# Layer 1's modulation rows issued in every third turn of layer 0's feed-forward network

## The chip, the cores and the metric

The kernel runs on one core of a Trainium2 chip. The metric is device time in microseconds (us) of one execution; the time quoted for the kernel before is the median of three runs.

PE is the matrix engine, PEld its weight loads, DVE the vector engine, ACT the scalar engine, POOL the general engine, and SP the engine whose queue issues the transfers between device memory and on-chip memory. Each engine works through its own list of instructions in order and waits for the others by semaphores. A "granted clock" of 1.00 is PE's full speed.

## The reference

Two transformer layers work on 512 latent tokens and 256 context tokens of width 1024, in float32. Each layer first makes six modulation vectors (shift, scale and gate, for the attention and for the feed-forward network), then runs attention and a feed-forward network with squared ReLU:

```python
for i in range(DEPTH):                                  # DEPTH = 2
    mod_x = jax.nn.silu(c) @ w_ada[i] + b_ada[i]        # c: 1024, w_ada[i]: 1024 x 6144
    mod_c = jax.nn.silu(c_ctx) @ w_ada[i] + b_ada[i]
    sh1, sc1, g1, sh2, sc2, g2 = jnp.split(mod_x[:, None, :], N_MOD, axis=-1)
    ...
    hx = x * (1.0 + sc1) + sh1
    hc = ctx * (1.0 + csc1) + csh1
    ax, ac = ...                                        # windowed attention, differential attention
    x = layer_norm(alpha * x + g1 * ax, ln1_g[i], ln1_b[i])
    fx = sqrelu_mlp(x * (1.0 + sc2) + sh2, mlp_w1[i], mlp_w2[i])
    x = layer_norm(alpha * x + g2 * fx, ln2_g[i], ln2_b[i])
    if need_ctx: ...                                    # the same for the context, layer 0 only
return x
```

The modulation vectors of layer 1 depend on nothing but `c`, `c_ctx`, `w_ada` and `b_ada`, so they can be made at any time before layer 1 wants them.

## The kernel before, in words

**Matrix products.** Every float32 product is made of three products of rounded operands: a weight tile `w` is split by ACT into a high part (`w_h`, a rounding copy, L264) and by DVE into a low part (`w_l = w - w_h`, L314), and `mm3` (L325 to L327) multiplies high by high, low by high and high by low. So each weight tile passes through four engines: SP loads it into a `w_raw` tile, ACT casts it, DVE subtracts, PE uses it. There are three `w_raw` tiles in the ring `rraw` (`NRAW = 3`) for layer 0.

**Layer 0's feed-forward network** (`mlp_pipe`) treats 768 tokens in six blocks of 128. The first product goes in sixteen "pairs" q of 256 hidden columns; from q = 3 on each pair takes seven half-size products of twelve matmuls (384 columns wide, tile `h_ps`; their weights are called `w_half`). Between these products stands the second product in small pieces: a "group" (tile `y_ps`) is one chunk c of hidden columns, one half of the output columns and one token block, and it is done in two half groups of six matmuls (512 columns wide). `steps(n)` lets n half groups run. Before q = 3 there are twelve, in each pair q = 3 to 13 twelve (4, 4, 4, 0), and in q = 14 and 15 six each.

**The filler.** `steps` calls `R.extra()` once after each half group, and `ahead()` calls it once in each pair. Those calls are named turns below: 12 + 11 x 12 + 2 x 6 = 156 from the half groups and 13 from the pairs, 169 in all. In layer 0 a turn takes the next step of the generator `filler`, which is `ada_rows`: it makes modulation vectors without PE. A step loads two rows of 128 x 512 of the transposed `w_ada` into a `w_raw` tile (tensor `in_w_adaT`, one 512 KB transfer), and DVE multiplies each with a broadcast copy of silu(c) (tile `cB`) and sums along the row (`tensor_tensor_reduce`, in the trace CUSTOM_DVE_ANT_0 with a DVE_READ_ACCUMULATOR2_ANT behind it). The last gate of layer 0 and the two vectors that layer 1's attention wants first are made for both latent and context tokens: such a piece has four of these DVE instructions ("double piece" below), the other vectors' pieces have two ("single piece"). The width is done in two halves; each half has one step that loads `cB`, then 12 double pieces, then 16 single pieces: 2 x (1 + 12 + 16) = 58 steps, with 160 DVE instructions.

When a gate vector is complete (m = 2 or 5), `ada_gate` turns it into rows: PE transposes it (`gate_t`, L456), ACT copies it (`gate_s`), SP stores it (`gate_d`). What the turns have not done is done where it is wanted: `need(...)` runs the generator on, in `g2` for layer 0's last gate, in `done2` for the first two vectors of layer 1, and after the whole feed-forward network for the rest of layer 1.

**What sets the order.** PE's order is written by a planner in the kernel (`Flow`): it keeps model times for the other engines and takes the job whose inputs are ready by that model. The other engines' orders, SP's too, come from the scheduler of the framework, which goes by program order and the tiles that are free. In the hardware each of these lists is worked off strictly in order, so a transfer that waits for a `w_raw` tile holds up all transfers behind it on SP, and a DVE instruction that waits for its transfer holds up all behind it on DVE.

Of the kernel before, what the change touches and what calls it, by code (L numbers as in the profile page):

```python
# [234 lines left out]
def hybrid_block(ctx: ExitStack, tc: tile.TileContext, t: dict, out: bass.AP):  # L235
# [373 lines left out]
    def tok_product(pool, src, W, seq, acc, gates, done=None, st=None, scale=1.0, extra=None, pre={}, sink=None,  # L609
# [5 lines left out]
        for i, (half, tb) in enumerate(seq):  # L615
# [41 lines left out]
            if extra is not None and tb < 4:  # L657
                next(extra, None)
# [802 lines left out]
    with tc.tile_pool(name="mlp0", bufs=1, reuse_waits="tile") as pool:  # L1461
# [26 lines left out]
        class R0:  # L1488
            rhalf = Ring(fl, 3)
            mixes = ((2, 2, 2, 0), (4, 4, 4, 0))  # L1490
            p3_first, gate_at, res = True, 16, None
            ahead, done = 1, 0

            def pair_raws(self):
                return [(x, None, None) for x in self.raws]
# [29 lines left out]
                    dma(D, [], out=acc[tb], in_=m_spill[tb])  # L1525

            def extra(self):
                next(filler, None)

        def main0():  # L1530
            yield from tok_product(pool, oT, {1: st1["W"]}, [(1, tb) for tb in range(NTB)], acc, (gx, gc), done1, st1,
# [42 lines left out]
        filler = ada_rows(pool, c_rows.rearrange("s k p -> s (k p)"))  # L1574
# [359 lines left out]
    with tc.tile_pool(name="mlp1", bufs=1, reuse_waits="tile") as pool:  # L1934
# [37 lines left out]
        class R1:  # L1972
            rhalf = Ring(fl, 4)
            mixes = ((1, 1, 1, 1), (2, 2, 2, 2))
            p3_first, gate_at, ahead = True, 10, 2
# [110 lines left out]
```

## Time and profile before

| | us |
|---|---|
| median of three runs (1687.13 to 1692.9) | 1690.02 |
| the profiled execution | 1690.94 |
| its span, first to last instruction | 1689.1 |
| PE busy | 1578.0 (93% of the span) |
| DVE busy | 1131.7 (67%) |
| ACT busy | 792.2 (47%) |
| POOL busy | 445.6 (26%) |
| mean granted PE clock | 0.975 |

The profile comes from one execution. Its page gives the busy time of each engine, the span in 40 slices of 42 us (each digit a busy share in tenths, with the granted PE clock and the share of the DMA engines below), and the chain of waits. Other views group the waits, list instructions in order of time, or give the busy times of chosen stretches; a row "(x158)" in such a stretch counts instructions. Matmuls overlap in the records, so PE can be shown busy throughout and yet do fewer of them: their count in a stretch says more than the busy time. Some matmul records can be missing (a few per cent).

### The profile page before, as it was taken

What the parts mean: (1) busy time and instruction counts of PE and PEld (TensorE: products, weight loads), DVE (VectorE), ACT (ScalarE), POOL (GpSimd) and SP (SyncE); (2) the same over time, 40 slices, a digit from 0 to 9 for tenths busy, and PEclk for the clock granted to TensorE, in tenths of its full rate; (3) what the DMA queues carried; (4) which work ended last, traced back from release to release, by engine and by line L of the source; (5) the groups of instructions that cost most, each with busy time, mean ns of one, the idle gap of its engine ahead of it and who ended that gap; (6) DMA issues with size and microseconds to landing.
All of it is one profiled execution on the core that took longest, in us unless ns stands there. A gap on an engine that the chain in (4) does not pass through costs nothing. (4 is left out here: it accounts for less than half of the span.)

```text
span 1689.1 us, 25129 instructions
## 1 busy us (share of the span) xinstructions
PE 1578.0 (93%) x9465; PEld 1388.1 (82%) x9465; DVE 1131.7 (67%) x2204; ACT 792.2 (47%) x1683; POOL 445.6 (26%) x364
## 2 busy tenths in 40 slices
PE   7899999999687899999999899999989899999997
PEld 5787777789576799899888899899877788999986
DVE  4655677698889864453567677777664975566687
ACT  3465675364222243342425555555552645555550
POOL 1333454114111112111281122220100023333463
PEclk9999999999798899999999999999999899999998
DMA  9111541543765722121143222211114233332331
GB/s 367 40 51 32 190 161 39 193 147 103 235 213 167 232 89 75 50 95 55 50 146 116 60 69 69 66 51 38 48 50 150 63 125 100 100 100 100 100 101 50
DMA packets 66433, 181.16 MB, mean 107 GB/s; under 512 B 7368, under 2 KB 13320, under 8 KB 66312
## 3 DMA queue, kind: packets, MB, share of 16 engines
q1 hardware_dynamic: 66312, 179.56, 31.6%
q8 instruction: 74, 1.21, 0.3%
q14 instruction: 47, 0.39, 0.1%
HBM read 168.49 MB, written 11.04 MB: 106 GB/s over the span
## 5 line engine op out<-in xcount | busy, mean ns | idle before, releaser
L325 PE MATMUL y_ps<-w_h,hid 128*128 128x512 f32 (+1 forms) x648 | 256.7, 396 | 27.3 <-ACT w_h L264 26.3
L326 PE MATMUL y_ps<-w_l,hid 128*128 128x512 f32 (+1 forms) x648 | 257.0, 397 | 10.1 <-DVE w_l L314 10.1
L327 PE MATMUL y_ps<-w_h,hid 128*128 128x512 f32 (+1 forms) x648 | 255.0, 394 | 0.0
L268 POOL TENSOR_TENSOR w_sum<-w_raw 128x512 f32<-128x512 f32 x52 | 94.8, 1822 | 501.5 <-DMA w_raw<-in_w 435.5
L314 DVE TENSOR_TENSOR w_l<-w_raw,w_h 128x1024 fp32r<-128x1024 f32 (+1 forms) x133 | 163.3, 1237 | 73.3 <-ACT w_h L264 72.7
L264 ACT CAST w_h<-w_raw 128x1024 fp32r<-128x1024 f32 (+1 forms) x133 | 131.7, 1001 | 146.7 <-PE y_ps L327 68.4
L325 PEld LDWEIGHTS y_ps<-w_h,hid 128*128 128x128 f32 x648 | 124.6, 192 | 52.4 <-ACT w_h L264 28.2
L260 DVE TENSOR_TENSOR w_half<-w_raw,w_half 128x512 fp32r<-128x512 f32 x130 | 103.9, 803 | 86.3 <-ACT w_half L264 86.0
L326 PEld LDWEIGHTS y_ps<-w_l,hid 128*128 128x128 f32 x648 | 124.5, 192 | 34.7 <-DVE w_l L314 12.7
L327 PEld LDWEIGHTS y_ps<-w_h,hid 128*128 128x128 f32 x648 | 124.5, 192 | 26.2 <-DVE hid L260 0.3
L264 ACT CAST w_half<-w_raw 128x512 fp32r<-128x512 f32 x130 | 79.8, 619 | 125.9 <-PE h_ps L327 75.4
L325 PE MATMUL qkv_ps<-w_h,hx 128*128 128x384 f32 (+1 forms) x384 | 128.9, 336 | 0.6 <-ACT qT L264 0.5
L326 PE MATMUL qkv_ps<-w_l,hx 128*128 128x384 f32 (+1 forms) x384 | 123.6, 322 | 0.0
L327 PE MATMUL qkv_ps<-w_h,hx 128*128 128x384 f32 (+1 forms) x384 | 123.5, 322 | 0.0
L260 DVE TENSOR_TENSOR fx<-y_ps,fx 128x512 f32<-128x512 f32 x110 | 75.6, 687 | 68.9 <-PE y_ps L327 68.5
L268 POOL TENSOR_TENSOR e<-e,sm 128x512 f32<-128x512 f32 (+2 forms) x96 | 92.6, 977 | 108.6 <-DVE sm L260 90.0
L264 ACT ACTIVATE relu<-relu 128x384 f32<-128x384 f32 (+3 forms) x104 | 69.5, 671 | 50.9 <-DVE relu L260 49.5
L268 POOL TENSOR_TENSOR rope<-rope,rope 128x256 f32<-128x256 f32 (+1 forms) x40 | 34.5, 862 | 213.5 <-DVE rope L260 170.0
L260 DVE CUSTOM_DVE_ANT_0 w_raw<-w_raw,cB 128x512 f32<-128x512 f32 x112 | 77.0, 725 | 12.5 <-DMA w_raw<-in_w_adaT 12.4
L264 ACT ACTIVATE e<-e,nm 128x513 f32<-128x513 f32 (+2 forms) x96 | 65.9, 687 | 32.8 <-DVE nm L260 26.0
L264 ACT COPY relu<-h_ps 128x384 f32<-128x384 f32 (+1 forms) x78 | 32.8, 421 | 92.9 <-PE h_ps L327 92.3
L325 PE MATMUL h_ps<-hx1m,w_half 128*128 128x256 f32 x260 | 73.0, 281 | 3.0 <-ACT relu L264 2.8
(266 smaller groups left out, 4280.4 us busy)
## 6 DMA issues: line engine op xcount, KB each, us to landing
w_raw<-in_w SPq DMA_DIRECT2D x128, 512.0 KB, 3.6
w_raw<-in_w_adaT SPq DMA_DIRECT2D x56, 512.0 KB, 4.5
w_raw<-in_w_ada SPq DMA_DIRECT2D x24, 512.0 KB, 4.3
w_raw<-in_b_w SPq DMA_DIRECT2D x32, 384.0 KB, 3.5
raw<-in_w_ada SPq DMA_DIRECT2D x16, 512.0 KB, 9.6
w_raw<-in_a_wq SPq DMA_DIRECT2D x8, 512.0 KB, 4.8
w_raw<-in_a_wo SPq DMA_DIRECT2D x8, 512.0 KB, 4.3
w_raw<-in_b_wo SPq DMA_DIRECT2D x8, 512.0 KB, 4.5
```

Source lines behind the costliest of these rows:

```text
L260: fn(**kw)
L264: fn(**kw)
L268: fn(**kw)
L314: last["split"] = nc.vector.tensor_tensor(**kw)
L325: nc.tensor.matmul(out=o, lhsT=lh, rhs=rh, start=start, stop=False, **kw)
L326: nc.tensor.matmul(out=o, lhsT=lh, rhs=rl, start=False, stop=False, **kw)
L327: last["pe"] = nc.tensor.matmul(out=o, lhsT=ll, rhs=rh, start=False, stop=stop, **kw)
```

## The change

`R0`, the class with layer 0's settings for the feed-forward network, counts its turns, and only every third turn takes a step of the filler. Nothing else is touched; layer 1's `extra` does nothing, as before. In 169 turns 56 of the 58 steps are taken. The last two pieces, both of layer 1's last gate (m = 5), are made by `need` after the feed-forward network, ahead of layer 1's attention.

```diff
@@ class R0 @@
             p3_first, gate_at, res = True, 16, None
-            ahead, done = 1, 0
+            ahead, done, turn = 1, 0, 0
...
             def extra(self):
-                next(filler, None)
+                self.turn += 1
+                if self.turn % 3 == 0:
+                    next(filler, None)
```

What this does to the engines' lists is seen at three places. The first is SP's list from where the filler's first loads stand, in the first half groups (`in_w_adaT` are the filler's loads, `in_w` the weights of the feed-forward network, `cB` the broadcast copies). Before:

```order
L275 DMA w_raw<-in_w_adaT 128x2x512 x11
L275 DMA w_raw<-in_w 128x1024
L275 DMA w_raw<-in_w_adaT 128x2x512 x3
L275 DMA w_raw<-in_w 128x1024 x2
L275 DMA w_raw<-in_w_adaT 128x2x512 x4
```

With the change:

```order
L275 DMA w_raw<-in_w_adaT 128x2x512 x3
L275 DMA w_raw<-in_w 128x1024
L275 DMA w_raw<-in_w_adaT 128x2x512 x2
L275 DMA w_raw<-in_w 128x1024
L275 DMA w_raw<-in_w_adaT 128x2x512
L275 DMA w_raw<-in_w 128x1024 x2
L275 DMA w_raw<-in_w_adaT 128x2x512
```

The weight load that stood behind eleven of the filler's loads stands behind three, and after that the two kinds alternate.

The second is SP's list where layer 0 ends and layer 1's attention begins (`x_spill` stores layer 0's result, `in_b_w` are weights of the attention, `cosT`, `sinT` and `lamv` its constants). Before:

```order
L1583 DMA x_spill<-acc_7898 128x1024
L275 DMA w_raw<-in_b_w 128x768 x4
L283 DMA c_cosT<-in_cosT 128x256
L283 DMA c_sinT<-in_sinT 128x256
L1605 DMA lamv<-in_lamv 128x256
```

With the change:

```order
L1585 DMA x_spill<-acc_7878 128x1024
L275 DMA w_raw<-in_b_w 128x768
L275 DMA w_raw<-in_w_adaT 128x2x512 x2
L275 DMA w_raw<-in_b_w 128x768 x3
L462 DMA gate_d_8621<-gate_s 8x128
L283 DMA c_cosT<-in_cosT 128x256
L283 DMA c_sinT<-in_sinT 128x256
L1607 DMA lamv<-in_lamv 128x256
```

The last two pieces' loads and the store of the gate made from them now stand ahead of the attention's constants.

The third is PE's list at the same border (`qkv_ps` are the attention's projections of the normalised tokens in `hx`, 384 columns for latent blocks and 256 for context blocks; `kT_ps` and `qT_ps` the first transposes of keys and queries). Before, the projections of the context blocks followed directly, and thirty matmuls later the first `kT_ps`:

```order
L325 MATMUL qkv_ps<-w_h,hx_8181 128x384
L326 MATMUL qkv_ps<-w_l,hx_8181 128x384
L327 MATMUL qkv_ps<-w_h,hx_8181 128x384
L325 MATMUL qkv_ps<-w_h,hx_8181 128x256
L326 MATMUL qkv_ps<-w_l,hx_8181 128x256
```

With the change:

```order
L326 MATMUL qkv_ps<-w_l,hx_8165 128x384
L327 MATMUL qkv_ps<-w_h,hx_8165 128x384
L456 MATMUL gate_t<-identr,mods_82 8x128
L1652 MATMUL kT_ps<-identr,sk 128x128 x2
L1667 MATMUL qT_ps<-identr,sq 128x128 x4
L325 MATMUL qkv_ps<-w_h,hx_8165 128x256
```

The gate's transpose has come to the border, and the first transposes of keys and queries now stand ahead of those thirty matmuls.

## The prediction, made before the changed kernel was run

> **What bounds the kernel now.** I read the page's slices first:
>
> ```profile
> PE   7899999999687899999999899999989899999997
> DVE  4655677698889864453567677777664975566687
> PEclk9999999999798899999999999999999899999998
> ```
>
> PE is busy nearly throughout, so what counts is where it is not. A slice is 42 us; slices 11 to 14 (422 to 591 us) are the one stretch inside layer 0 where PE's digit and its clock drop together, and DVE's digit rises to 8 and 9 there. So I cut the feed-forward network at the starts of its pairs (the times are where each pair's fourth `h_ps` product begins):
>
> ```profile
> core 0: us, PE busy (x) PEld busy (x) DVE busy (x) ACT busy (x) POOL busy (x), PEclk, DMA share, GB/s
> 402.90:463.60 60.70, 46.27 (x206) 38.92 (x205) 53.79 (x141) 16.84 (x30) 6.29 (x4) 0.86 0.59 195
> 463.60:504.10 40.50, 34.53 (x158) 29.94 (x156) 32.84 (x77) 11.72 (x20) 4.98 (x3) 0.92 0.66 214
> 504.10:548.70 44.60, 34.60 (x158) 30.02 (x158) 42.24 (x107) 12.70 (x21) 6.61 (x4) 0.89 0.52 168
> 548.70:592.20 43.50, 36.34 (x157) 31.12 (x158) 36.53 (x93) 12.12 (x20) 7.18 (x5) 0.88 0.71 229
> 592.20:623.40 31.20, 31.20 (x159) 28.22 (x157) 17.03 (x23) 13.69 (x22) 6.18 (x4) 1.00 0.25 82
> ...
> 624.70:780.70 156.00, 156.00 (x783) 141.30 (x782) 73.99 (x101) 61.24 (x96) 28.27 (x20) 1.00 0.21 68
> ```
>
> The same work of some 158 matmuls takes 31.2 us in the fifth row and in each of the five pairs of the last (156.0 / 5), but 40.5 to 44.6 us in rows two to four. The slow stretch is exactly the filler's:
>
> ```profile
> L260 DVE CUSTOM_DVE_ANT_0 w_raw<-w_raw,cB x112: 675/685/1778, 404.5 to 590.0; 128x512 f32<-128x512 f32 x112
> L260 DVE CUSTOM_DVE_ANT_0 ada_pr<-w_raw,cB x48: 669/686/1780, 402.4 to 541.4; 128x512 f32<-128x512 f32 x48
> ...
> 402.90:592.20 189.30, 111.27 (x160) 0.88 0.61 201
> ```
>
> Its first instruction starts at 402.4, its last at 590.0; the third row is DVE's busy time in the filler's instructions alone, 111.27 us for 160, 0.70 us each. And PE's waits in this stretch, then one of them followed back in the timelines of PE, ACT and SP:
>
> ```profile
> PE y_ps L325 <- ACT w_h L264: 26.3, 4, 11.9
> PE y_ps L326 <- DVE w_l L314: 7.4, 5, 2.4
> PE h_ps L327 <- DVE w_half L260: 3.6, 1, 3.6
> ...
> 438.67 0.80 PE L325 MATMUL y_ps<-w_h,hid 128*128 128x512 f32 x1 [11.87 <-ACT w_h L264]
> ...
> 437.57 1.04 ACT L264 CAST w_h<-w_raw 128x1024 fp32r<-128x1024 f32 x1 [13.30 <-DMA w_raw<-in_w]
> ...
> 393.57 37.58 SPq L275 DMA_DIRECT2D w_raw<-in_w_adaT  x11
> 433.83 0.34 SPq L275 DMA_DIRECT2D w_raw<-in_w  x1
> ```
>
> PE waited 11.87 us for a weight whose load SP issued only at 433.83, behind eleven loads of the filler that took 37.58 us to get out, because each needs one of three `w_raw` tiles and those are freed at DVE's pace. So **the filler's rate is the bound here**: it outruns DVE, and through the shared tiles and SP's order DVE's backlog becomes PE's wait.
>
> **What the stretch loses.** Three pairs at 31.2 would take 93.6 us. The first row holds the twelve opening half groups and a pair less its last two products:
>
> ```profile
> 402.92 0.39 PE L325 MATMUL y_ps<-w_h,hid 128*128 128x512 f32 x1
> 419.24 0.34 PE L325 MATMUL h_ps<-hx0m,w_half 128*128 128x384 f32 x1
> ```
>
> The opening ran undisturbed, 16.3 us for its 72 matmuls. A pair has 72 such and 84 of `h_ps`, so those 84 take 31.2 - 16.3 = 14.9 and 24 of them 4.3; the first row would take 16.3 + 31.2 - 4.3 = 43.2. Together 136.8 of the 189.3 us shown: **the filler costs 52.5 us**, waits (37.6 by the three rows and a last one of 0.3) and, for the rest, the halved clock after them.
>
> **The change, term by term.** *The filler's work stays* (160 instructions, 56 loads of 512 KB), but its rate falls to a third. Per pair of 31.2 us DVE has 73.99 / 5 = 14.8 us of its own. Thirteen double pieces (2.8 us each at 0.70) added 36.4 before: 51.2, far over 31.2; thirteen single pieces added 18.2: 33.0, still over. At 13/3 pieces it is 14.8 + 12.1 = 26.9 (86%) with double and 14.8 + 6.1 = 20.9 (67%) with single pieces. The order shows SP's loads alternating. So the backlog has no cause left, and I credit the whole **-52.5**.
>
> *What is left of it.* Near 86% an in-order DVE will sometimes be late. The weights of the next half groups have this room:
>
> ```profile
> 653.45 1.05 ACT L264 CAST w_h<-w_raw 128x1024 fp32r<-128x1024 f32 x1 [1.73 <-PE y_ps L327]
> ...
> 656.28 1.22 DVE L314 TENSOR_TENSOR w_l<-w_raw,w_h 128x1024 fp32r<-128x1024 f32 x1
> ...
> 663.03 0.39 PE L325 MATMUL y_ps<-w_h,hid 128*128 128x512 f32 x1
> ```
>
> The cast can only begin when PE has finished with the old tile (653.45), the second subtraction ends at 657.5 and PE wants it from 663.0: 5.5 us of room, two double pieces. Lower bound 0. Upper bound: one double piece, 2.8 us, late in each of the eleven pairs, 31. The nearest row is `w_l`'s, 7.4 us in 5 waits, 1.5 each; one such in each of the 5.5 pairs in which double pieces now fall (24 pieces by 3 turns by 1/13) makes **+8**.
>
> *The border of the layers.* The last two single pieces (four DVE instructions, 2.8 us) fall where DVE has a gap, so they cost nothing themselves; if that gap were gone, 2.8. What does cost is what is queued behind the gate's store on SP, and PE's new order:
>
> ```profile
> 924.37 0.43 SPq L283 DMA_DIRECT2D c_sinT<-in_sinT  x1
> 924.85 1.83 SPq L1605 DMA_DIRECT2D lamv<-in_lamv  x1
> ...
> 935.60 0.76 DVE L260 TENSOR_TENSOR hx<-hx_v,hx 128x256 fp32r<-128x256 f32 x2 [5.29 <-ACT hx L264]
> ...
> 938.18 0.28 PE L325 MATMUL qkv_ps<-w_h,hx 128*128 128x256 f32 x1
> 941.61 0.28 PE L327 MATMUL qkv_ps<-w_h,hx 128*128 128x256 f32 x1
> 945.03 0.37 PE L1650 MATMUL kT_ps<-identr,sk 128*128 128x128 f32 x2 [3.15 <-DVE nlam L1613]
> ...
> L462 SPq DMA_DIRECT2D gate_d<-gate_s x4: 303/496/675, 187.2 to 595.4; - x4
> ...
> DMA to landing us min/median/max: 4.7/4.7/4.7
> ```
>
> The 5.29 us before the `hx` row is that gap. The constants went out at 924 and were long there. Now the transpose of the gate follows the projection that ends at 938.2; 0.5 us for it and ACT's copy, 0.5 for the store's issue, 4.7 for cosT to land (the last row is its own), some 0.8 more for sinT and lamv behind it: 944.7. From there the old chain from lamv's first use to the first `kT_ps`:
>
> ```profile
> 941.73 0.28 DVE L1607 TENSOR_TENSOR lamp<-lamv 128x128 f32<-128x128 f32 x1
> 944.69 0.29 DVE L260 TENSOR_TENSOR sk<-rope,sk 128x128 fp32r<-128x128 f32 x1 [0.35 <-ACT sk L264]
> ```
>
> is 3.3 us to PE's 945.03. It held a `w_l` of 0.96, which now stands later: about 2.4, so `kT_ps` at 947.1, 2.1 later than before, and the thirty matmuls that ran from 938.2 to 941.9 (3.7 us) are still to do: +5.8. Part of them fills later waits, so I take **+5**; bounds 0 (all of them do) and 10 (lamv lands 4 us later still).
>
> The clock after a wait shows here:
>
> ```profile
> 438.60:444.60 6.00, 4.92 (x11) 0.51 0.77 255
> 944.90:949.30 4.40, 4.26 (x27) 0.65 0.31 94
> ```
>
> It was 0.51 after the 11.87 us wait and already 0.65 after 3.15. The Trainium skill (TensorE: Matmul & The Clock Gate, section "HAM oscillation — how this bites in real kernels") states that PE gaps above about 3.4 us put it back to half clock, each gap anew. By that rule the scattered waits of the +8 cost only themselves, while the new border gap is charged another 1.7 (an estimate: half of 3.4), which speaks against the change; the sum would be 1653. The trace puts the drop no later than 3.15 us, and the old border paid it too.
>
> **The sum**, against the profiled execution's 1690.94 us (span 1689.1, 1.8 around it; 0.9 over the median of 1690.02): 1690.9 - 52.5 + 8 + 5 = **1651**, -2.3%.
>
> **Rivals.** *Everything comes free* (0.16): nothing is late at 86% and the border fills up: 1690.9 - 52.5 + 0 to 5, about 1640. For it: the pairs after 592.2 have not one us of idle PE. Against: they had DVE at 47%.
>
> *DVE waits for the filler's loads* (0.18). DVE no longer lags, so it may stand at a piece whose load has not landed:
>
> ```profile
> DVE w_raw L260 <- DMA w_raw<-in_w_adaT: 12.4, 14, 1.8
> ```
>
> At 1.8 us, the longest of these, per piece, a pair with double pieces needs 26.9 + 7.8 = 34.7, 3.5 over 31.2, in 5.5 pairs 19; single ones (28.7) still fit. With the +8 and +5: about 1670.
>
> *The stretch is slow for another reason*, its own sums for one, and the change only moves the filler (0.08): 1690.9 + 0 to 5, no change. Against it: the pace returns with the filler's last instruction, not with any sum.
>
> *SP's order holds a weight load in every pair* (0.08), the one that ends slower. Weights and filler share three tiles, and SP takes the next weight as soon as one is free:
>
> ```profile
> 655.79 3.16 SPq L275 DMA_DIRECT2D w_raw<-in_w  x3
> ```
>
> If a filler's load waits for a tile ahead of that weight, PE waits as it did for `w_h`, 26.3 / 4 = 6.6 us each time. Once in each of eleven pairs is 72: 1690.9 - 52.5 + 72 + 5 = 1715. It decides from (52.5 - 5) / 11 = 4.3 us per pair. For it: two of three tiles hold weights from 656 to about 685, nearly a whole pair. Against: in the new order never more than three of the filler's loads stand before a weight.
>
> **Numbers.** The forecast has 0.50. Faster by over 0.3% (5 us, about what this kernel's measurement can tell from none): 0.50 + 0.16 + 0.18 = 0.84; within it 0.08; slower 0.08. The range takes in the free case and the DVE waits with the bounds of the +8 and +5: 1636 to 1684, leaving out the last two and the fringes, 0.2.
>
> **What would show it.** Right: in the windows the pairs from q = 3 to 13 take 31 to 33 us at a clock near 1.00; `y_ps <- ACT w_h` falls from 26.3 us to a few; the filler's 160 instructions run from 402 to about 930; the first `kT_ps` waits 7 to 10 us. The DVE rival: `in_w_adaT` waits on DVE of 50 us or more and double-piece pairs near 35. SP's rival: `w_h` waits of 4 us in most pairs. The forecast is wrong if the pairs beyond 592 slow by more than 3 us each, or if the border costs over 10.

## The result

| | before | with the change |
|---|---|---|
| median (same chip) | 1690.64 us | 1663.78 us (1661.15 to 1666.47) |
| ratio, 95% interval | | 0.9843 (0.9816 to 0.987) |
| span of the profiled execution | 1689.1 | 1664.6 |
| PE busy / DVE busy | 1578.0 / 1131.7 | 1574.4 / 1130.1 |

The change makes the kernel 26.9 us faster, 1.6%. The prediction was 1651, 39 us faster: the direction and the cause of the gain came out, but nearly a third of the forecast gain did not come.

The slices of the changed kernel; those of before stand at the head of the prediction:

```profile
PE   7899999989899999999998999999989899999997
DVE  4655677698675668767476777677664975556577
PEclk9999999999999999999999999999899999999998
```

The dip of PE and its clock in slices 11 to 14 is gone, and DVE's 8 and 9 there are 5 to 7, spread to slice 21. The feed-forward network, cut at the same marks as in the prediction (start of the opening, then each pair's fourth `h_ps` product, q = 3 to 13; each row has the stretch, its length, then busy time and instructions of each engine):

```profile
core 0: us, PE busy (x) PEld busy (x) DVE busy (x) ACT busy (x) POOL busy (x), PEclk, DMA share, GB/s
403.49:452.88 49.39, 43.79 (x206) 37.32 (x205) 34.44 (x84) 16.20 (x29) 5.81 (x4) 1.00 0.39 128
452.88:485.64 32.76, 32.76 (x156) 29.87 (x157) 25.91 (x53) 13.84 (x23) 4.86 (x4) 0.95 0.51 161
485.64:518.83 33.19, 31.25 (x157) 28.01 (x155) 20.61 (x41) 10.72 (x19) 5.19 (x4) 1.00 0.45 143
518.83:552.90 34.07, 33.40 (x157) 29.78 (x157) 22.45 (x43) 13.63 (x21) 6.78 (x5) 0.95 0.43 140
552.90:584.08 31.18, 31.18 (x158) 28.28 (x157) 20.86 (x37) 12.28 (x19) 6.17 (x4) 1.00 0.42 135
584.08:615.16 31.08, 31.08 (x158) 28.20 (x156) 20.41 (x41) 12.17 (x19) 3.87 (x3) 1.00 0.38 119
615.16:646.83 31.67, 31.43 (x157) 28.23 (x156) 26.82 (x54) 12.04 (x19) 8.00 (x5) 1.00 0.34 116
646.83:678.66 31.83, 31.49 (x159) 28.11 (x157) 26.42 (x57) 11.02 (x20) 6.09 (x4) 1.00 0.41 134
678.66:713.50 34.84, 31.57 (x157) 28.01 (x157) 23.20 (x52) 11.87 (x20) 4.47 (x4) 1.00 0.43 136
713.50:747.56 34.06, 33.47 (x158) 29.78 (x158) 23.17 (x50) 13.77 (x22) 6.77 (x5) 0.95 0.46 155
747.56:778.74 31.18, 31.18 (x158) 28.29 (x157) 23.08 (x42) 11.04 (x18) 6.17 (x4) 1.00 0.43 135
```

The first row was 60.7, the next three 40.5, 44.6 and 43.5. Now it is 49.4, and the pairs take 31.1 to 34.8. From the opening to the mark of q = 13 (402.92 to 810.55 before, 403.49 to 778.74 now) the stretch has shrunk from 407.6 to 375.3 us. Undisturbed it would take 355.2, as two experiments below show for its two parts. So the filler cost 52.4 us before and costs **20.0** now. PE's idle time is 12.6 of it: 49.39 less 43.79, and 7.05 in the ten pairs, whose PE busy time is 318.81 of 325.86. (The expectations below put what the stretch loses at 12.8 us; that is near this idle time alone, and the 20.0 counts the halved clock too.)

The loss does not lie where the double pieces are. In a double piece two of the four sums write a tile `ada_pr`; on DVE such sums number 17, 7, 0, 0, 0, 4, 8, 8, 4, 0 and 0 in these rows. The two pairs fullest of them, at 615.16 and 646.83, lose 0.5 and 0.6 us at 83 to 85% of DVE. The opening loses 6.1, and the pairs at 485.64, 518.83, 678.66 and 713.50, with few double pieces or none, lose 2.0, 2.9, 3.6 and 2.9 at 62 to 68%.

What PE waited for between 400 and 1000, and DVE for the filler's loads (us in total, times, longest):

```profile
PE h_ps L325 <- DVE relu L260: 11.5, 5, 3.4
PE kT_ps L1652 <- DVE sk L260: 7.2, 1, 7.2
PE y_ps L326 <- DVE w_l L314: 4.9, 2, 2.7
...
DVE w_raw L260 <- DMA w_raw<-in_w_adaT: 36.6, 25, 4.1
DVE ada_pr L260 <- DMA w_raw<-in_w_adaT: 30.2, 15, 3.7
```

The 26.3 us of `y_ps <- ACT w_h` are not in this list any more. In their place DVE stands at the filler's pieces until their loads land: 66.8 us, where it was 13.9. The filler now starts its last instruction at 904.0:

```profile
L260 DVE CUSTOM_DVE_ANT_0 w_raw<-w_raw,cB x112: 675/689/1787, 405.6 to 904.0; 128x512 f32<-128x512 f32 x112
```

Four of PE's waits in the stretch are over 1 us: 2.24, 3.36, 1.95 and 2.82. They are of two kinds. The longest, in DVE's and PE's timelines at the end of the first row:

```profile
451.65 0.69 DVE L260 CUSTOM_DVE_ANT_0 ada_pr<-w_raw,cB 128x512 f32<-128x512 f32 x1 [3.65 <-DMA w_raw<-in_w_adaT]
452.27 0.55 DVE L260 TENSOR_TENSOR relu<-h_ps,relu 128x384 f32<-128x384 f32 x1
...
452.88 0.44 PE L325 MATMUL h_ps<-hx0m,w_half 128*128 128x384 f32 x1 [3.36 <-DVE relu L260]
```

DVE stood 3.65 us for a load, made one product, and only then the `relu` sum that PE was waiting for. The 2.24 us wait, in the opening, ends behind a piece that stood 2.63 for its load. The other two end behind a weight. The 1.95 us wait, in SP's, POOL's, DVE's and PE's timelines (POOL's `w_sum` is made from a loaded weight tile, and a `w_half` from it):

```profile
506.74 0.38 SPq L275 DMA_DIRECT2D w_raw<-in_w_adaT  x1
507.34 5.38 SPq L275 DMA_DIRECT2D w_raw<-in_w  x2
512.31 1.30 POOL L268 TENSOR_TENSOR w_sum<-w_raw 128x512 f32<-128x512 f32 x1 [25.35 <-DMA w_raw<-in_w]
...
517.02 0.69 DVE L260 TENSOR_TENSOR w_half<-w_sum,w_half 128x512 fp32r<-128x512 f32 x1 [4.07 <-ACT w_half L264]
...
518.83 0.62 PE L325 MATMUL h_ps<-hx0m,w_half 128*128 128x384 f32 x1 [1.95 <-DVE relu L260]
```

The weight went out right behind a load of the filler, and POOL could begin 5.0 us after its issue; without a filler (`no filler` below) the weight of this place goes out at 502.75 with no such load ahead, and POOL begins 3.6 us later. From there the chain runs through POOL, ACT and DVE to the `relu` sum that stands behind `w_half` on DVE. The 2.82 us wait at 713.50 has the same chain (DVE stood 5.21 for `w_half`), with two of the filler's sums, 1.2 us, between `w_half` and `relu` besides.

**The whole difference of the spans**, -24.5 us: the stretch -32.4; the opening begins 0.6 later; the pair of q = 13 takes 26.13 in place of 24.84, +1.3 (PE waits 3.05 for a `relu` sum, before 1.76); from there to the end 859.7 in place of 853.7, +6.0.

### The profile page after: what moved, and what is told of

It reads as the page before. It is cut to its first block, busy times and chain, and to the rows that moved or that the text cites. A ratio compares the mean times of both kernels' runs of the same rounds, so it can differ in the third digit from the quotient of the medians.

```text
span 1664.6 us, 25124 instructions
## 1 busy us (share of the span) xinstructions
PE 1574.4 (95%) x9465; PEld 1388.4 (83%) x9465; DVE 1130.1 (68%) x2204; ACT 791.4 (48%) x1683; POOL 443.1 (27%) x364
## 5 line engine op out<-in xcount | busy, mean ns | idle before, releaser
L326 PE MATMUL y_ps<-w_l,hid 128*128 128x512 f32 (+1 forms) x648 | 252.5, 390 | 4.9 <-DVE w_l L314 4.9
L325 PE MATMUL y_ps<-w_h,hid 128*128 128x512 f32 (+1 forms) x648 | 252.3, 389 | 1.2 <-DVE g_tmp L583 1.2
L327 PE MATMUL y_ps<-w_h,hid 128*128 128x512 f32 (+1 forms) x648 | 251.5, 388 | 1.0 <-DVE hid L260 1.0
L327 PEld LDWEIGHTS y_ps<-w_h,hid 128*128 128x128 f32 x648 | 122.2, 189 | 27.3 <-DVE hid L260 1.9
L325 PEld LDWEIGHTS y_ps<-w_h,hid 128*128 128x128 f32 x648 | 122.2, 189 | 23.8 <-DVE g_tmp L583 1.4
L325 PE MATMUL h_ps<-hx0m,w_half 128*128 128x384 f32 x208 | 73.5, 353 | 11.5 <-DVE relu L260 11.5
```

The source lines that it names most:

```text
L325: nc.tensor.matmul(out=o, lhsT=lh, rhs=rh, start=start, stop=False, **kw)
L326: nc.tensor.matmul(out=o, lhsT=lh, rhs=rl, start=False, stop=False, **kw)
L327: last["pe"] = nc.tensor.matmul(out=o, lhsT=ll, rhs=rh, start=False, stop=stop, **kw)
```

## The experiments

Single executions of one kernel differ by up to 12 us here, and the start of the opening alone lay between 402.3 and 409.7 us in the profiles below, though nothing ahead of it was changed. So each kernel stands with its median and its ratio to the kernel before on the same chip (the rows were not all taken on one chip, so the ratios compare better), and the mechanism is read from the stretch between the marks in its profile, from the opening to q = 13. The last columns are that stretch, what it is above 355.2, and DVE's waits for the filler's loads:

| kernel | median | ratio (95%) | stretch | above 355.2 | DVE waits for loads |
|---|---|---|---|---|---|
| before | 1690.64 | 1 | 407.6 | 52.4 | 13.9 |
| the change | 1663.78 | 0.9843 (0.9816 to 0.987) | 375.3 | 20.0 | 66.8 |
| no filler | 1648.85 | 0.9744 (0.9722 to 0.9766) | 360.9 | 5.7 | - |
| small sums | 1650.17 | 0.9751 (0.9719 to 0.9783) | 357.9 | 2.7 | 92.1 |
| no loads | 1663.7 | 0.9839 (0.9807 to 0.9871) | 371.9 | 16.7 | - |
| no loads, held | 1663.31 | 0.9834 (0.9817 to 0.9851) | 363.4 | 8.2 | - |
| held | 1663.91 | 0.9847 (0.9825 to 0.987) | 373.5 | 18.3 | 26.6 |
| done early | 1665.98 | 0.9842 (0.9819 to 0.9864) | 375.4 | 20.2 | 71.0 |
| load ahead | 1670.82 | 0.9885 (0.9865 to 0.9906) | 370.2 | 15.0 | 19.4 |
| load ahead, 3 of 8 | 1668.84 | 0.9863 (0.9843 to 0.9882) | 381.9 | 26.7 | 23.5 |
| by work | 1670.97 | 0.987 (0.9848 to 0.9892) | 382.9 | 27.7 | 84.4 |
| every second | 1677.43 | 0.9912 (0.9891 to 0.9933) | 390.4 | 35.2 | 45.9 |
| before, small sums | 1671.05 | 0.9885 (0.9863 to 0.9907) | 387.1 | 31.8 | 61.4 |
| before, no loads | 1677.2 | 0.991 (0.9886 to 0.9933) | 397.9 | 42.7 | - |

No whole kernel here is faster than the change.

### Without a filler, without its loads, without its sums

`no filler` takes both of these edits, `no loads` the first, `small sums` the second:

```diff
-                    raw, rg, rr = raw_tile()
-                    d = dma(1024, [rg], out=raw..., in_=t["w_adaT"][...])
+                    d = None
...                                                # src = cB[0]; every sum writes an ada_pr tile
-                            src = raw[:, i * 512:i * 512 + 512]
+                            src = raw[:, i * 512:i * 512 + 16]
...
-                            d = dv(512, ..., out=to, in0=src, in1=cB[s], ...)
+                            d = dv(16, ..., out=to, in0=src, in1=cB[s][:, 0:16], ...)
```

> The changed kernel with the filler's substance out: no loads of w_adaT, and each of its 160 multiply-and-sum instructions works on 16 columns of the broadcast copy instead of 512 of the weights, so that layer 1's modulation vectors (and layer 0's last gate) are not computed; turns and steps stay. Both theories: the opening takes 43.2 us and the pairs 31.2 each, so the feed-forward network loses nothing to the filler. The pairs of the changed kernel lost about 20 us by its windows, so 1664 - 20 = 1644, and the border (first kT_ps late) stays as it is or is shorter by the two loads that are missing. If the pairs were slow for a reason of their own, the time stays at 1664.

> The changed kernel without the 56 loads of w_adaT; the 160 instructions keep their size and multiply the broadcast copy with itself, so layer 1's modulation vectors and layer 0's last gate are not computed. DVE's work is as before, while no raw tile, no place in SP's queue and no landing is waited for. Theory A (what is left in the pairs is the loads: DVE stands 66.8 us at pieces whose load has not landed, and weight loads stand behind the filler's on SP): the pairs fall to 31.2 to 31.8, the whole to 1644 to 1650. Theory B (it is DVE's time, 86% in pairs with double pieces, the +8 of the prediction): the pairs stay at 32 to 35, the whole at 1660 to 1665.

> The changed kernel with all 56 loads, but each multiply-and-sum takes the first 16 of the 512 columns only, so DVE's 111 us of filler fall to some 15, and the modulation vectors are sums over a part. Theory A (loads): DVE still stands at each piece until its load has landed, and weight loads still stand behind the filler's; what is left is 15 to 20 us of the pairs' 20, so 1655 to 1664. Theory B (DVE's time): the pairs fall to 31.2 to 31.8, the whole to 1644 to 1650.

Without a filler the kernel takes 1648.85, 43 us less than before by the ratio, and 15 (by the medians) to 17 (by the ratios) less than the change. Its ten pairs:

```profile
454.07:765.99 311.92, 311.92 (x1564) 282.31 (x1563) 149.86 (x200) 123.21 (x193) 57.85 (x40) 1.00 0.21 68
```

The opening row of `small sums`:

```profile
409.70:452.99 43.29, 43.29 (x206) 37.59 (x205) 17.17 (x80) 16.87 (x27) 5.17 (x4) 1.00 0.50 166
```

43.3 and 311.9 make the 355.2 used above: the undisturbed stretch of the prediction (43.2 and 31.2 a pair) was measured right. No run shows both parts at once. `no filler` lost 5.7 in its own opening, and that is a remnant of the filler too:

```profile
426.92 0.17 DVE L260 CUSTOM_DVE_ANT_0 ada_pr<-cB 128x16 f32<-128x16 f32 x1 [3.23 <-DMA cB<-c_rows]
...
429.79 0.50 PE L326 MATMUL y_ps<-w_l,hid 128*128 128x512 f32 x1 [3.77 <-DVE w_l L314]
```

With no loads to hold them, all but four of the 160 short sums were drawn into the opening, and DVE stood 3.23 us at one of them for the second half's `cB`, ahead of the `w_l` that PE wanted.

With small sums nearly the whole loss went: 2.7 left of 20.0, though DVE stood for loads longer than ever, 92.1 us. Standing alone costs PE next to nothing. That seemed to decide for theory B, the more so as taking out the loads brought nothing at all (1663.7). But `no loads` had changed more than it should, as its rows show:

```profile
454.31:488.29 33.98, 33.36 (x157) 29.77 (x157) 33.98 (x81) 13.17 (x22) 5.81 (x4) 0.95 0.21 70
...
590.99:623.74 32.75, 32.75 (x157) 29.84 (x158) 15.34 (x23) 13.48 (x21) 3.85 (x3) 0.95 0.20 65
```

DVE is busy for 33.98 of 33.98 us, then 15.3: with no load to wait for, the scheduler had drawn the pieces forward and was done with all but the last two (four instructions at the border) by 591. The third-turn rule places the pieces in the program; the order on DVE is the scheduler's, and only the loads and tiles hold the pieces back. So this run is a kernel with the filler at full speed again, and says something else: at nearly 100% of DVE its pairs lose 2 to 5 us, not the 9 to 13 of before.

### The two causes in the kernel before

The same two edits, each made to the kernel before:

> The kernel before with all loads issued at every turn, but each multiply-and-sum takes the first 16 of 512 columns, so the modulation vectors are sums over a part. By the prediction DVE's pace is the root: eleven loads held SP for 37.58 us because DVE freed the tiles slowly. Then the loads go out as fast as they land, the weights are no longer held, and most of the 52.5 us comes back: 1645 to 1660. If instead the loads themselves (56 of 512 KB in a row ahead of the weights) were the cause, little changes: 1675 to 1690.

> The kernel before without the 56 loads of w_adaT; the 160 instructions keep their size, multiply the broadcast copy with itself, and stand at every turn (modulation vectors not computed). With 16-column sums and all loads the kernel before still lost 25 of the 44.5 us that the filler costs there, so loads and DVE's time each seem to carry about half. If the two halves add, what stays here is DVE's half, some 20 us: 1691 - 25 = 1666. If DVE's backlog costs only through the raw tiles and SP's order, as the prediction told it, then without loads nothing is held and the time is that without a filler, 1649. If DVE's time bounds the stretch alone (its 165 us of work in the 189 us), it is 1670 or more.

Small sums took 20.6 of its 52.4 us away, no loads 9.7. Neither is near the 1649 of no filler, so neither DVE's time nor the loads carry it alone. With small sums the loads still crowd SP: eight of them stand around one weight load, the last five for 8.34 us,

```profile
434.85 0.34 SPq L275 DMA_DIRECT2D w_raw<-in_w  x1
436.20 8.34 SPq L275 DMA_DIRECT2D w_raw<-in_w_adaT  x5
```

and `y_ps <- ACT w_h` is still 5.6 us and `h_ps <- ACT w_half` 5.0. Eleven loads had taken 37.58 in the kernel before: DVE's pace did make SP's queue slow, but the queue costs without it too. Without loads what is left is DVE's backlog alone: PE waited 11.9 us for one `relu` sum, and 14.3 for the sums of a gate that it was to transpose, in a pair that took 52.2. So a full DVE costs a pair anything from 2 to 21 us, by what PE wants from behind the backlog.

### The border, and other paces

```diff
-                if self.turn % 3 == 0:
+                if self.turn % 3 == 0 or self.turn in (164, 167):      # done early
+                if self.turn % 2 == 0:                                 # every second
+                if self.turn >= self.due:                              # by work: yield 2 * n (1 for cB)
+                    self.due = self.turn + next(filler, 1)
```

> The changed kernel with two more turns (164 and 167) on which a step is taken, so that all 58 steps are done inside the feed-forward network and no load, sum or gate store of the filler stands at the border of the layers. If the border costs what the prediction put on it (+5), the first kT_ps waits about 3 us instead of 7.17 and the whole falls by 3 to 5 us, to 1659 to 1661. If what was lost after the pairs has another cause, it stays at 1664.

> Steps spread by DVE's work: after a double piece the next step waits four turns, after a single piece two, after a broadcast copy one; 24 x 4 + 32 x 2 + 2 = 162 of 169 turns, so nothing is left for the border. DVE then has 14.8 + 13/4 x 2.8 = 23.9 us of work per pair with double pieces and 14.8 + 13/2 x 1.4 = 23.9 with single ones, 77%. If what is left is DVE's time (16-column sums took 11 of the 12.8 us away), the pairs at 77% lose about half a us each as those with 67% did: 12.8 falls to 5, the border gives 3 to 5: 1651 to 1656. If the number of loads per pair counted, the single-piece pairs with 6.5 loads would now be the slow ones and the whole stay at 1660 to 1664.

> Every second turn takes a step: done after 116 turns. Pairs with double pieces have 14.8 + 6.5 x 2.8 = 33.0 us of DVE work, over the 31.2 of PE; those with single pieces 23.9. If DVE's time decides, the double-piece pairs (3.7 of them, and the opening) take 34 to 38 us, 25 us are lost in place of 12.8, and the border gives 3 to 5 back: 1668 to 1672. If DVE's time isn't what decides, about 1660.

*Done early* did what it says at the border, where the first `kT_ps` waits 3.15 as before. But the two pieces now cost as much in the pair of q = 13, which takes 31.4 us (780.27 to 811.63) in place of 26.1:

```profile
791.55 0.69 DVE L260 CUSTOM_DVE_ANT_0 w_raw<-w_raw,cB 128x512 f32<-128x512 f32 x1 [3.07 <-DMA w_raw<-in_w_adaT]
794.07 1.82 DVE L260 TENSOR_TENSOR hid<-relu,hid 128x768 fp32r<-128x768 f32 x2
...
795.08 0.80 PE L327 MATMUL y_ps<-w_h,hid 128*128 128x512 f32 x1 [2.37 <-DVE hid L260]
```

Four products stand between the first of these rows and the second. So the border's price was moved, not saved: 1665.98.

*By work* missed by 15 to 20 us. The even 77% of DVE that it planned did not come (60 to 83% of a pair in the trace, since the scheduler places the pieces), and the pairs lost more than those of the change. Two of them took 38.3 and 37.5 us: in the first PE waited 2.51 us for a `hid` that stood behind a piece that had stood 2.58 for its load, in the second 3.20 for a late `w_half`, the other kind of wait. This kernel also has the longest standing of those with whole sums, 84.4 us. DVE's mean share does not tell what a pair loses; what stands late ahead of something PE wants soon does. *Every second* turn cost 35.2 in the stretch, against 25 expected, with pairs of 31.4 to 38.9.

### Pieces held at their turns, and loads sent ahead

```diff
+                            hold = last.get("pe") if s == 0 and i == 0 else None
-                            d = dv(512, [d], nc.vector.tensor_tensor_reduce, ...)
+                            d = dv(512, [d], behind(nc.vector.tensor_tensor_reduce, hold), ...)
```

*Load ahead* also makes the sums of a piece one step after its load (`late` keeps one piece):

```diff
+                    if late:
+                        sums(*late.pop())
                     raw, rg, rr = raw_tile()
                     d = dma(...)
+                    late.append((h, l, m, k, cB, mod, n, raw, rr, d))
                     yield
```

and its second version steps where `turn * 3 // 8` grows.

> As the run without loads (sums of the broadcast copy with itself, modulation vectors not computed), but the first instruction of each piece also waits for the last matmul that PE was given before that turn. Without loads the scheduler had pulled all pieces forward: they were done by 591, DVE at 98 to 100% until then, so that run took the change itself away with the loads and told nothing of them. Held to their turns, DVE's work per pair is that of the changed kernel. Theory A (what is left is DVE standing for loads): the pairs take 31.2 to 32, 1647 to 1653. Theory B (DVE's time at 86%): the double-piece pairs take 32 to 35, 1658 to 1664.

> The changed kernel, whole, with that one wait added: the first sum of each piece waits for PE's last matmul before its turn. In the changed kernel the scheduler runs the pieces up to twelve instructions ahead of their turns (33 of them stand before the third relu sum of the stretch, 21 when held), and DVE stands 66.8 us at them for loads. Theory A: held back, most loads have landed when DVE comes to them; the waits for loads fall below 30 us and the 12.8 us that the stretch loses to the filler fall to about 5: 1655 to 1658. Theory B: nothing changes, 1662 to 1666. If a raw tile that is held longer keeps weights out, it gets slower: 1670.

> The changed kernel with the sums of a piece made one step (three turns, some 7 us) after its load was issued, held as above; a 59th step is needed for the last sums, so three steps are left for the border. Theory A: no piece is met before its load has landed (landing takes 3.8 us): waits for loads near 0, pairs 31.2 to 32, the stretch loses 1 to 4 us in place of 12.8; the border costs 4 to 6 as before: 1652 to 1656. Theory B: 1662 to 1666. If the raw tile held for three turns starves the weights, w_h waits come back and it is slower than 1666.

> The same with three steps in eight turns in place of three in nine, so that all 59 are done in the feed-forward network. DVE has 14.8 + 13 x 3/8 x 2.8 = 28.5 us of work in pairs with double pieces, 91%. Theory A: DVE's share does not matter as long as it stands at nothing; pairs 31.2 to 32.5, and the border gives 3 to 5 back: 1648 to 1653. Theory B: the double-piece pairs get worse than in the changed kernel: 1664 to 1668.

*Held, without loads.* DVE's work now lies as the prediction had it, and the opening and first seven pairs run almost undisturbed, those planned at 86% of DVE too (82% at most in the trace); the last three lose 7, two of them all of it:

```profile
406.37:449.69 43.32, 43.32 (x206) 37.58 (x205) 32.65 (x69) 18.57 (x31) 6.18 (x4) 1.00 0.15 49
449.69:669.09 219.40, 219.00 (x1095) 197.54 (x1094) 163.03 (x304) 84.99 (x135) 42.34 (x28) 1.00 0.21 70
669.09:769.78 100.69, 96.07 (x471) 86.04 (x469) 71.95 (x148) 36.08 (x58) 16.77 (x12) 0.98 0.19 63
```

So DVE's time alone is worth 8.2 us, the loads without it 2.7, both together 20.0. The 8.2 is not quite DVE's time alone either: the pieces also stood 16.9 us for the matmuls that they were held to, and 1.9 of the last pairs' loss is a wait behind a late `w_sum` with two sums between, as at 713.50 above, though no load of the filler was there. The profiled execution took 1656.18, but the kernel's three others 1663 to 1664, as long as the change itself; this split therefore rests on one trace, and the times don't confirm it.

*Held, with loads*, theory A should have paid: DVE's standing for loads fell from 66.8 to 26.6 us, though the pieces then stood 11.2 us for the matmuls that they were held to. Yet 18.3 of the 20.0 us stayed. What PE waits for instead:

```profile
503.54 0.38 SPq L275 DMA_DIRECT2D w_raw<-in_w_adaT  x1
510.35 0.69 DVE L673 CUSTOM_DVE_ANT_0 w_raw<-w_raw,cB 128x512 f32<-128x512 f32 x1
511.07 0.33 SPq L275 DMA_DIRECT2D w_raw<-in_w  x1
515.47 1.05 ACT L264 CAST w_h<-w_raw 128x1024 fp32r<-128x1024 f32 x1 [4.13 <-DMA w_raw<-in_w]
519.22 0.69 PE L325 MATMUL h_ps<-hx0m,w_half 128*128 128x384 f32 x1 [2.74 <-ACT w_half L264]
```

The load went out at 503.54; its tile was used by DVE, at its turn, from 510.35. The next weight left SP at 511.07, ACT stood 4.13 us for it with the `w_half` cast behind, and PE 2.74 for that. *Load ahead* gave the same in larger form: standing 19.4, the stretch 15.0, better by 5; but with three steps left for the border, `kT_ps` waits 8.42 us there, and the mark of q = 13 to the first `kT_ps` takes 149.4 in place of 139.2. With 3 steps in 8 turns that went, and the stretch lost 26.7, with `y_ps <- ACT w_h` waits of 2.04 and 2.13.

So it seems that the three `w_raw` tiles are what is short: either the tile is asked for late, and DVE stands at the piece, or early, and a weight stands in SP's queue. This is an inference: a tile of the filler's own was not tried, and weights that take longer to land beside a load of the filler (5.0 against 3.6 us above) would cost with more tiles too.

## Why the prediction was right, and where it was not

*The bound and the -52.5.* Right. The undisturbed stretch of 355 us was found in the experiments (43.3 and 311.9), the filler's share of before is 52.4, and the `w_h` waits went with the change. Its chain (DVE slow, tiles held, SP late) is less than half of it: with the sums cut to 16 columns 31.8 of the 52.4 us remained, with the loads still crowding SP.

*"In each of the 5.5 pairs ... makes +8".* This is the step that failed, in size and in place: 20.0 were measured. DVE's busy time per double-piece pair was right (26.9 forecast; 26.82, 26.42 in the two fullest), but those pairs lost 0.5 and 0.6 us, less than the 1.5 of the sum; the opening and the pairs behind the double pieces lost the rest. That DVE's time alone came to 8.2 in one trace is luck: 7 of it lay in two pairs, not 1.5 in each of 5.5. What the sum left out is, first, the standing: 1.8 us was the longest wait for a filler's load in the trace of before, and 4.1 after, 66.8 in all. Two of the four long waits, 5.6 of 10.4 us, end behind such a piece. The prediction had this as a rival with 19 more. Its first sign, 50 us or more, appeared; its second, double-piece pairs near 35, did not. The measured 1663.8 lies between the two forecasts of 1651 and 1670, nearer to the rival. Second, "never more than three of the filler's loads stand before a weight" did not make that harmless: the other two long waits, 4.8 us, end behind a weight that was late, and in the held kernel this kind is the larger. Third, the clock: the three waits of 3.36, 1.95 and 2.82 us were each followed by a window at half speed, 1.7 us each, 5.1 of the 20.0, while the prediction let scattered waits cost only themselves.

*The border, +5.* The sequence came as forecast, in PE's, SP's and DVE's timelines:

```profile
910.54 0.27 PE L456 MATMUL gate_t<-identr,mods 128*8 128x128 f32 x1
911.13 0.30 SPq L462 DMA_DIRECT2D gate_d<-gate_s  x1
913.57 0.42 DVE L260 TENSOR_TENSOR rope<-qkv_ps,c_cosT 128x256 f32<-128x256 f32 x1 [1.79 <-DMA c_cosT<-in_cosT]
915.37 0.29 DVE L1609 TENSOR_TENSOR lamp<-lamv 128x128 f32<-128x128 f32 x1 [1.37 <-DMA lamv<-in_lamv]
917.98 0.50 PE L1652 MATMUL kT_ps<-identr,sk 128*128 128x128 f32 x2 [7.17 <-DVE sk L260]
```

The wait is 7.17, inside the 7 to 10; from the transpose to `kT_ps` it is 7.4 us where 8.9 were forecast, since cosT, issued at 911.52, was there about 2 us later, not 4.7. Of the +6.0 behind q = 13, 3.4 are two half-speed windows behind waits of 3.05 and 2.66 us, which leaves 2.6 for the border itself. That the last two pieces "fall where DVE has a gap" held; taken earlier they cost five.

*The rivals.* "Everything comes free" held to within 0.7 us for five of the ten pairs (31.1 to 31.8), the two fullest of double pieces among them, and not for the opening and the other five. "SP's order" did not turn the sign, but its mechanism is one side of what is left. "Another reason" fell with `no filler`. The mark set for a wrong forecast, over 3 us in each pair beyond 592, was passed by one pair alone (34.8, where the second half's double pieces end).

## What to carry to other kernels

Work that fills gaps on an in-order engine is not priced by that engine's mean share: look at what stands behind each piece in the queue, and add the wait for its load to its duration. Where fillers and critical loads share a few tiles, as here, a slower filler helped (52.4 to 20.0 us), while asking for the filler's loads earlier mostly moved the wait from one queue to the other (18.3 and 15.0 stayed). And an experiment that takes a wait away must show that the order stayed: without its loads this filler ran where it liked.

## What the runs showed of the hardware

**The clock goes by windows of 3.41 us on a fixed grid.** In the trace of the change the half-speed stretches begin at 454.08, 518.94, 713.50, 805.66 and 843.21: 19, 57, 27 and 11 times 3.413 us apart. What decides is PE's idle share in the window before, by the recorded matmuls; here two successive windows of the change (length, PE busy, matmuls, clock):

```profile
515.52:518.93 3.41, 1.46 (x8) 1.00 0.00 0
518.93:522.35 3.42, 3.42 (x11) 0.50 0.02 5
```

and two of before:

```profile
871.12:874.53 3.41, 1.96 (x8) 1.00 0.27 64
874.53:877.95 3.42, 3.42 (x16) 1.00 0.13 51
```

The wait in the first row was 1.95 us and all in one window, 57% of it: the next window ran at 0.50. The wait of before, in the first of its rows, was longer, 2.69 us, but lay across a border, 42% of this window: no drop. Counted on this grid from 400 to 1640 us of all fourteen profiles: of 98 full-speed windows with 55% or more idle 97 were followed by half speed, of 281 with 20 to 52% only 23, most of those near 50%, and of some 2150 with less than 20% none; between 52 and 55% both happened. A window at half speed that was idle for 18% or more was followed by another (56 of 56); of 138 with less, 124 were followed by full speed. So a wait of 2 to 3.4 us costs itself, and 1.7 us more if it happens to fill over half a window. The Trainium skill (TensorE: Matmul & The Clock Gate, section "What's actually happening") gives the free-running window of 3413 ns, and the trace agrees. The Trainium skill, in the same section, lets the clock drop after at least one idle window; here 1.95 us of idle time in one window were enough.

**A product on DVE beside a sum on POOL can take over twice as long.** In the run without loads POOL was at its sums from 512.85 on: DVE's product at 512.12 took 0.69 us, the one at 514.72 took 1.66, and POOL's sum at 514.21 took 1.62 in place of 1.29. In the change 8 of the filler's 160 instructions were lengthened so (1.06 to 1.79 us), and five others that ran mostly beside a sum on POOL kept 0.68 to 0.69, so it is a small part here and not the rule.
